# Tile starts at multiples of 64 bytes, and the delta rule's block transfers moved, in a four-layer decoder trunk on one core

## The chip, the cores and the metric

The kernel runs on one core of a Trainium2 chip. The metric is device time in microseconds of one execution. Before the change the median of three runs is 1248.63 us (1247.71 to 1249.18). The profile comes from one further execution, of 1247.2 us, whose instructions span 1245.1 us. Engines are named PE (matmuls; PEld is the weight load that overlaps them), DVE, ACT, POOL (GpSimd) and SP, which here only issues DMAs.

## The reference

The input is 256 positions of 1024 features in float32. Four layers follow; layer i uses mixer i mod 3 and then a convolutional feed-forward part, each with a norm before it and a residual sum after it:

```
for i in range(DEPTH):                       # DEPTH = 4
    h = rmsnorm(x, mix_norm[i])
    # i % 3: 0 = block attention, 1 = gated short convolution, 2 = gated delta rule
    x = x + mixer(h)
    x = x + conv_ffn(rmsnorm(x, ffn_norm[i]), w_up, conv_w, w_down)
return rmsnorm(x, final_norm)

def conv_ffn(h, w_up, conv_w, w_down):       # 1024 -> 2 x 2816 -> 1024
    u = causal_dwconv(h @ w_up, conv_w)
    return (silu(u[..., :FFN_DIM]) * u[..., FFN_DIM:]) @ w_down
```

So layers 0 and 3 are attention, layer 1 is the short convolution and layer 2 is the gated delta rule. In the delta rule each of 8 heads has queries, keys and values (after a convolution of width 4 and silu), and per chunk of positions it solves a unit lower triangular system:

```
a_mat = where(strict, (k_beta @ k.T) * decay, 0)
t_mat = triangular_solve(a_mat + eye, eye)   # the inverse
u, w = t_mat @ v_beta, t_mat @ (k_beta * exp(gc))
# then over the chunks, in order:
v_new = u_i - w_i @ state
o_i   = q_i @ state + a_i @ v_new
state = state * sd_i + k_i.T @ v_new
```

Its output is normalised per head, gated by silu(z) and multiplied by an output matrix.

## The kernel before

Activations stand transposed, features on partitions: `x` is 8 blocks of 128 features by 256 positions. The large matrix products keep float32 accuracy by splitting both operands into a rounded high part and the rest. A product of a weight tile with `x` is three matmuls (high x high, high weights x low, low weights x high). Where high and low activations stand side by side in one tile (`xs`, `aw`, `yw`), it is two: 512 columns against the high weights and 256 against the low ones. All operands of these are of the type that PE takes in one pass.

**The weights** come as one stream of 404 chunks of 8 tiles (128x128) each, in the order of use (class `Stream`, lines 104 to 168). SP issues the loads into four buffers `wraw`; ACT rounds a chunk to `whi` (line 152) and DVE takes the difference `wlo` (line 153), up to five chunks ahead of PE. All of SP's DMAs stand in one queue and are issued in its order: an issue that waits for a semaphore holds everything behind it, the weight loads too.

**The order of PE's work** is written out by hand by a planner (class `Weave`, lines 171 to 215). A `fill` generator brings the large products tile by tile, each tile adding 0.327 to the planner's clock. Beside it run steps, generators that yield a pair: what the PE work just emitted adds to the clock, and how much clock must pass, or which named events must be set, until the step goes on. Whatever is due is emitted after the current tile; where the fill has to wait for an event, the clock is moved on without PE work. PE executes exactly this order, and an instruction whose data isn't there holds all behind it. The order on the other engines and DMA queues is made by the framework's scheduler. The helper `after` (line 267) ties an instruction to the last emitted matmul in that scheduler, as an order only, without a semaphore.

**The delta rule** (function `gdn`, line 600) takes the heads in two halves of four. Its fill is 16 jobs of 16 tiles, `q0` to `q7` (queries and keys), then `v` (values) and `z` (gates) for two heads each, then the output product, which needs `o0` (first half's heads) for its first half and `o1` for its second. Each half runs through these steps:

- `lengths` (711): transposes of queries and keys, squares. It waits for `L_QK` after a head's activation.
- `systems` (745): the four heads' triangular matrices into `aq`. At its end SP stores their key part to DRAM (line 766).
- `invert` (775): SP reads the 16x16 diagonal blocks back as `bl` (781). POOL inverts them row by row into `xb` (789 to 794). SP stores `xb` to DRAM (796) and reads it back in another shape as `xc` (799). After `L_BLOCKS` and `L_JOIN` on the planner's clock DVE multiplies it into `xt32` (802). `xb` and `bl` have one buffer, so the second half's elimination follows the first's.
- `join16` (811) and `join_half` (848): DVE transposes 32x32 squares to `xi32` (809), PE joins inverse blocks to 32, 64 and 128 rows.
- the rest of `half` (941): two chunks are solved one after the other, with PSUM copied by ACT or DVE between the products; `finish` (917) normalises each chunk (ACT squares, POOL's root at 928, DVE's scaling at 931, PE's transposes, ACT's copy at 936), and `output` (999) gates and splits it for the output product.

The tiles are taken from pools in the order in which the code names them; a tile's size is its last dimension in bytes. The pool `keep` begins with `x`, `xh`, `xl`, then `pv`, `cs`, `half8`, `warm`, `idle`; the pools of the weights, of small temporaries and of each layer part come behind it.

Of the kernel before, what the change touches and what calls it, by code (L numbers as in the profile page):

```python
# [9 lines left out]
F32 = mybir.dt.float32  # L10
# [5 lines left out]
P = 128  # L16
# [4 lines left out]
H = 8  # L21
# [17 lines left out]
SCALED = 5  # L39
LAG = 1.75  # L40
L_HEAD, L_SOFTMAX, L_TURN, L_MIX, L_READY = 3.5, 9.0, 1.0, 2.5, 0.5
L_QK, L_V, L_LEN, L_SYS, L_BLOCKS, L_JOIN, L_XI, L_PM, L_OUT = 6.0, 6.0, 1.0, 0.5, 6.0, 13.0, 1.0, 2.5, 1.0


PV_MIX = 0
# [6 lines left out]
PV_N = PV_GN + 1  # L52
# [12 lines left out]
C_N = C_ST + 2 * H  # L65
# [153 lines left out]
def trunk(ctx: ExitStack, tc: tile.TileContext, xT, wstream, pvec, cst, wba, hv, out):  # L219
    nc = tc.nc  # L220
    V, S, G = nc.vector, nc.scalar, nc.gpsimd

    keep = ctx.enter_context(tc.tile_pool(name="keep", bufs=1))
    wpool = ctx.enter_context(tc.tile_pool(name="wpool", bufs=1))
    psum = ctx.enter_context(tc.tile_pool(name="psum", bufs=1, space=PSUM))
# [3 lines left out]
    xht = keep.tile([P, KB, T], F32R, name="xh")  # L229
    xlt = keep.tile([P, KB, T], F32R, name="xl")  # L230
    xh, xl = [[z[:, k, :] for k in range(KB)] for z in (xht, xlt)]
    pv = keep.tile([P, PV_N], F32, name="pv")
    cs = keep.tile([P, C_N], F32, name="cs")
    xg = []
    half8 = keep.tile([P, 2, 8], F32, name="half8")

    V.memset(half8[:, 0], -0.5)
    V.memset(half8[:, 1], 0.5)
    warm = keep.tile([P, 8], F32, name="warm")
    S.activation(warm, half8[:, 0], AF.Square)  # L240
    ws = Stream(nc, wpool, wstream, wstream.shape[0])
    nc.sync.dma_start(out=pv[:, :PV_SC], in_=pvec[:, :PV_SC])
# [24 lines left out]
    def after(inst):  # L267

        tc.add_manual_dep(inst.ins, PE.last.ins.name, mybir.DependencyInfo(
            mybir.DependencyClass.NoSync, mybir.DependencyReason.SCHED_ONLY), reason="a DMA's latency")  # L270
# [5 lines left out]
    def bank(tag, bufs=4):  # L276
        return psum.tile([P, 512], F32, name=tag, bufs=bufs)
# [322 lines left out]
    def gdn(gain):  # L600
        nm = Norm()
        NS = 2 * G_H
        with tc.tile_pool(name="gdn", bufs=1) as pool, \
# [8 lines left out]
            V.tensor_sub(ws2[:, :, 2 * H:], wb, ws2[:, :, :2 * H].bitcast(F32))  # L612
            bt = pool.tile([P, 2, H], F32, name="bt")
            g = pool.tile([P, 2, H], F32, name="g")
            gc = pool.tile([P, 3, H], F32, name="gc")
            dl = pool.tile([P, H], F32, name="dl")
            eg = pool.tile([P, H], F32, name="eg")
            neg = pool.tile([P, H], F32, name="neg")
# [2 lines left out]
            def big(dt=F32):  # L621
                return pool.tile([P, NS, P], dt, name="big", bufs=NB)
# [122 lines left out]
            def systems(s):  # L745

                s.aq = pool.tile([P, NS, 2, P], F32, name="aq", bufs=2)
                yield 0, (f"d{s.h0}",)
                for a in range(G_H):
                    y = s.y[a]  # L750
                    pk = bank("sm")
                    for t in range(2):
                        ts = slice(t * P, (t + 1) * P)
                        PE.matmul(pk[:, t * T:(t + 1) * T], lhsT=y[:, 1, ts], rhs=y[:, 0:2, ts],
                                  start=True, stop=True)
                    for t in range(2):
                        m = 2 * a + t
                        V.scalar_tensor_tensor(s.aq[:, m], pk[:, t * T:(t + 1) * T].rearrange(
                            "p (q i) -> p q i", q=2), s.sk[:, m:m + 1],
                            s.dt[:, a, t, :].unsqueeze(1).to_broadcast([P, 2, P]), op0=ALU.mult, op1=ALU.mult)  # L760
                    yield 0.87, 0.5 * LAG

                nb = P // BLK
                row = (BLK * P + BLK) * nb
                d1 = dram.tile([NS * row], F32, name="d1")
                nc.sync.dma_start(
                    out=d1.rearrange("(m x) -> m x", m=NS)[:, :P * P].rearrange("m (p c) -> p m c", p=P),
                    in_=s.aq[:, :, 1, :])
                s.d1 = d1

                s.am = big()
                V.tensor_mul(s.am, s.aq[:, :, 1, :],
                             cs[:, C_UP:C_UP + P].unsqueeze(1).to_broadcast([P, NS, P]))

            def invert(s):

                nb, d1 = P // BLK, s.d1

                bl = pool.tile([NS * nb, BLK, BLK], F32, name="bl", bufs=1)
                with nc.allow_non_contiguous_dma(reason="16 values of a block's row"):  # L780
                    nc.sync.dma_start(
                        out=bl, in_=d1.rearrange("(q y) -> q y", q=NS * nb)[:, :BLK * P]
                        .rearrange("q (j c) -> q j c", j=BLK)[:, :, :BLK])
                xb = pool.tile([NS * nb, BLK, BLK], F32, name="xb", bufs=1)
                xm = pool.tile([NS * nb, BLK, BLK], F32, name="xm", bufs=1)
                G.memset(xb, 0.0)
                G.memset(xb.rearrange("p j i -> p (j i)")[:, ::BLK + 1], 1.0)
                yield 0, L_BLOCKS
                G.tensor_scalar(xb[:, 0, 1:], bl[:, 0, 1:], -1.0, None, op0=ALU.mult)
                for k in range(1, BLK - 1):  # L790
                    n, r = k + 1, BLK - 1 - k
                    G.tensor_mul(xm[:, :n, :r], xb[:, :n, k:k + 1].to_broadcast([NS * nb, n, r]),  # L792
                                 bl[:, k:k + 1, k + 1:].to_broadcast([NS * nb, n, r]))
                    G.tensor_sub(xb[:, :n, k + 1:], xb[:, :n, k + 1:], xm[:, :n, :r])  # L794
                d2 = dram.tile([NS, nb, BLK, BLK], F32, name="d2")
                nc.sync.dma_start(out=d2.rearrange("m b j i -> (m b) j i"), in_=xb)
                xc = pool.tile([P, NS, BLK], F32, name="xc", bufs=1)
                with nc.allow_non_contiguous_dma(reason="16 values of a block's row"):
                    nc.sync.dma_start(out=xc, in_=d2.rearrange("m b j i -> (b j) m i"))
                s.xt32 = pool.tile([P, NS, 2, BLK], F32, name="xt32", bufs=2)  # L800
                yield 0, L_JOIN
                after(V.tensor_mul(s.xt32, xc.unsqueeze(2).to_broadcast([P, NS, 2, BLK]),
                                   cs[:, C_EO:C_EO + 2].unsqueeze(1).unsqueeze(3).to_broadcast([P, NS, 2, BLK])))
# [137 lines left out]
            def half(s):  # L941
                yield from lengths(s)
                yield 0, L_SYS
                yield from systems(s)
                yield from invert(s)
                yield from join16(s)
                yield from join_half(s, 32, (0, 64), (0,), lambda r, m: s.xi32[r, m, :],
# [87 lines left out]
    for l in range(DEPTH):  # L1035
        kind = l % 3
        subs.append((lambda g, l=l, kind=kind: moba(g) if kind == 0 else sconv(g) if kind == 1
                     else gdn(g), PV_FFN + l * KB))
        subs.append((lambda g, l=l: ffn(l, g), PV_MIX + (l + 1) * KB if l + 1 < DEPTH else None))
# [97 lines left out]
```

## Time and profile before

| | |
|---|---|
| median of three runs | 1248.63 us (1247.71 to 1249.18) |
| profiled execution | 1247.2 us |
| its span | 1245.1 us |
| PE busy | 1225.7 us, 98% of the span |
| PEld busy | 1127.5 us, 91% |
| DVE busy | 982.9 us, 79% |
| ACT busy | 775.5 us, 62% |
| POOL busy | 104.4 us, 8% |
| DMA | 215.80 MB, mean 173 GB/s |

The span's times count from its first instruction. Matmuls are pipelined: one that lasts 0.28 us starts some 0.12 us after the one before it, so the distance from start to start is what a stream of them costs, and PE counts as busy throughout. Idle time is listed with what ended it. The chain of work that ended last is followed back from the last instruction, at each step to what released it. The delta rule's part of the trace runs from about 578 us (its first tile) to 756 us (the last tile of its output product).

### The profile page before, as it was taken

The page shows a single profiled execution, that of the slowest core. Times are in us where ns is not written, and L with a number is a line of the kernel's source. Part 1 is how long each engine was busy: PE and PEld are TensorE (multiplying, and loading weights), DVE is VectorE, ACT ScalarE, POOL GpSimd, SP SyncE. Part 2 cuts the span into 40 slices and gives each one's busy share as a digit, 9 for nine tenths or more (in the row PEclk, how much of TensorE's full clock was granted, in tenths as well). Part 3 has the DMA queues.
Part 4 walks back from the last instruction along what each step waited for, and adds up shares of the span by engine and source line. Part 5 has one row for each costly group of instructions (what it writes and reads, how often), then busy time and mean ns, then how long its engine had stood idle before and what let it go on. Part 6 is the DMA issues. An engine that isn't in the chain of part 4 may idle for free.

```text
span 1245.1 us, 22068 instructions
## 1 busy us (share of the span) xinstructions
PE 1225.7 (98%) x8366; PEld 1127.5 (91%) x8366; DVE 982.9 (79%) x1720; ACT 775.5 (62%) x1427; POOL 104.4 (8%) x147
## 2 busy tenths in 40 slices
PE   9999999999999999999997999999999999999997
PEld 8989988889999988889997999988889989988886
DVE  6756999966878999866995668999775756999952
ACT  6655777644445777645873666777554655777641
POOL 2002000001002000001045102000011002000000
PEclk9999999999999999999998999999999999999998
DMA  8544465655555465655344244555655444466650
GB/s 289 200 153 166 146 201 186 213 188 189 176 182 186 153 201 193 200 189 183 126 131 126 90 136 137 200 192 189 208 190 175 156 161 165 145 202 188 211 177 34
DMA packets 67418, 215.80 MB, mean 173 GB/s; under 512 B 11248, under 2 KB 14832, under 8 KB 67312
## 3 DMA queue, kind: packets, MB, share of 16 engines
q1 hardware_dynamic: 67024, 213.86, 52.3%
q8 instruction: 66, 1.08, 0.3%
q10 hardware_dynamic: 288, 0.52, 0.1%
q14 instruction: 40, 0.33, 0.1%
HBM read 212.13 MB, written 2.23 MB: 172 GB/s over the span
## 4 chain that ended last, share of the span: by engine, by line
PE 89%; DVE 4%; ACT 2%; DMA 2%; issue 1%; POOL 1%; SPq 0%; POOLq 0%; DVEq 0%; ACTq 0%
PE mm L254 72%; PE sm L254 16%; DVE wlo L153 2%; DMA wraw<-wstream 1%; PE sm L257 1%; DVE xl L292 1%; ACT whi L152 1%; DVE yqk L422 1%; POOL xb L794 1%; POOL xm L792 1%; ACT jk L729 0%; DMA bl<-d 0%; DVE x L392 0%; DVE big L692 0%; DMA xc<-d 0%
## 5 line engine op out<-in xcount | busy, mean ns | idle before, releaser
L153 DVE TENSOR_TENSOR wlo<-wraw,whi 128x1024 fp32r<-128x1024 f32 (+1 forms) x404 | 489.5, 1212 | 155.7 <-ACT whi L152 154.0
L152 ACT CAST whi<-wraw 128x1024 fp32r<-128x1024 f32 (+1 forms) x404 | 420.2, 1041 | 290.9 <-PE mm L254 239.5
L254 PE MATMUL mm<-xh,whi 128*128 128x256 f32 x1024 | 296.5, 290 | 0.2 <-ACT whi L152 0.2
L254 PE MATMUL mm<-xh,wlo 128*128 128x256 f32 x1024 | 289.1, 282 | 1.2 <-DVE wlo L153 1.2
L254 PE MATMUL mm<-xl,whi 128*128 128x256 f32 x1024 | 288.7, 282 | 0.7 <-DVE xl L292 0.7
L254 PE MATMUL mm<-xs,whi 128*128 128x512 f32 x704 | 248.3, 394 | 0.0
L254 PE MATMUL mm<-aw,whi 128*128 128x512 f32 x704 | 247.3, 393 | 0.0
L254 PE MATMUL mm<-aw,wlo 128*128 128x256 f32 x704 | 199.1, 283 | 0.0
L254 PE MATMUL mm<-xs,wlo 128*128 128x256 f32 x704 | 199.1, 283 | 0.0
L254 PEld LDWEIGHTS mm<-xh,wlo 128*128 128x128 f32 x1024 | 193.5, 189 | 2.3 <-DVE wlo L153 2.1
L254 PEld LDWEIGHTS mm<-xl,whi 128*128 128x128 f32 x1024 | 193.8, 189 | 1.8 <-DVE xl L292 1.1
L254 PEld LDWEIGHTS mm<-xh,whi 128*128 128x128 f32 x1024 | 193.7, 189 | 1.4 <-ACT whi L152 0.4
L254 PEld LDWEIGHTS mm<-aw,whi 128*128 128x128 f32 x704 | 132.2, 188 | 30.6
L254 PEld LDWEIGHTS mm<-xs,whi 128*128 128x128 f32 x704 | 132.2, 188 | 30.5
L422 DVE SCALAR_TENSOR_TENSOR y<-u,pv,y 128x255 f32<-128x255 f32 (+1 forms) x352 | 149.0, 478 | 0.4
L254 PE MATMUL sm<-xs,whi 128*128 128x512 f32 x384 | 135.7, 393 | 0.0
L306 POOL TENSOR_TENSOR sq<-sq 128x256 f32<-128x256 f32 x62 | 53.3, 859 | 974.6 <-ACT sq L304 972.8
L254 PEld LDWEIGHTS mm<-xs,wlo 128*128 128x128 f32 x704 | 132.4, 188 | 0.0
L254 PEld LDWEIGHTS mm<-aw,wlo 128*128 128x128 f32 x704 | 132.3, 188 | 0.0
L254 PE MATMUL sm<-xs,wlo 128*128 128x256 f32 x384 | 108.6, 283 | 0.0
L420 ACT ACTIVATE y<-u,pv 128x256 f32<-128x256 f32 x176 | 81.4, 504 | 11.9 <-DVE u L451 6.6
L254 PEld LDWEIGHTS sm<-xs,whi 128*128 128x128 f32 x384 | 72.1, 188 | 16.6
(210 smaller groups left out, 1509.5 us busy)
## 6 DMA issues: line engine op xcount, KB each, us to landing
wraw<-wstream SPq DMA_DIRECT2D x396, 512.0 KB, 3.4
wraw<-wstream SPq DMA_DIRECT2D x8, 256.0 KB, 4.8
x<-xT SPq DMA_DIRECT2D x8, 128.0 KB, 4.7
d<-aq SPq DMA_DIRECT2D x2, 512.0 KB, 3.7
out<-xg ACTq DMA_DIRECT2D x2, 256.0 KB, 2.5
cs<-cst SPq DMA_DIRECT2D x1, 329.0 KB, 6.4
pv<-pvec SPq DMA_DIRECT2D x1, 324.5 KB, 4.9
cs<-cst SPq DMA_DIRECT2D x1, 320.0 KB, 5.9
```

What stands on the lines that cost most here:

```text
L152: self.nc.scalar.copy(hi[:, s], raw[:, s])
L153: self.nc.vector.tensor_sub(lo[:, s], raw[:, s], hi[:, s].bitcast(F32))
L254: self.last = nc.tensor.matmul(*a, **k)
L257: self.last = nc.tensor.transpose(*a, **k)
L292: V.scalar_tensor_tensor(xl[n], xn, col(gain + n), xh[n].bitcast(F32), op0=ALU.mult, op1=ALU.subtract)
L306: G.tensor_add(sums[0], sums[0], sq)
L420: S.activation(y, u, AF.Copy, scale=col(taps[0]))
L422: V.scalar_tensor_tensor(y[:, d:], u[:, :T - d], col(c), y[:, d:], op0=ALU.mult, op1=ALU.add)
L792: G.tensor_mul(xm[:, :n, :r], xb[:, :n, k:k + 1].to_broadcast([NS * nb, n, r]), bl[:, k:k + 1, k + 1:].to_broadcast([NS * nb, n, r]))
L794: G.tensor_sub(xb[:, :n, k + 1:], xb[:, :n, k + 1:], xm[:, :n, :r])
```

## The change

Sizes that put later tiles off a multiple of 64 bytes are rounded up to 16 floats (`even`): `pv`, `cs`, `warm`, and `gc` gets a fourth plane. In the delta rule POOL issues the store of its own rows instead of SP; the store of `aq` and the read of `xc` are tied to the last emitted matmul with `after`; two new yields, `L_STORE` and `L_ROWS + L_BACK`, stand before them on the planner's clock; and the constants change: `L_QK` 6.0 to 7.5, `L_XI` 1.0 to 2.0, `L_JOIN` 13.0 to 3.5, with the new `L_STORE` 2.0, `L_ROWS` 16.0, `L_BACK` 2.0.

```
-L_QK, L_V, L_LEN, L_SYS, L_BLOCKS, L_JOIN, L_XI, L_PM, L_OUT = 6.0, 6.0, 1.0, 0.5, 6.0, 13.0, 1.0, 2.5, 1.0
+L_QK, L_V, L_LEN, L_SYS, L_XI, L_PM, L_OUT = 7.5, 6.0, 1.0, 0.5, 2.0, 2.5, 1.0
+L_STORE, L_BLOCKS, L_ROWS, L_BACK, L_JOIN = 2.0, 6.0, 16.0, 2.0, 3.5
...
+    def even(n):
+        return -(-n // 16) * 16
...
-    pv = keep.tile([P, PV_N], F32, name="pv")
-    cs = keep.tile([P, C_N], F32, name="cs")
+    pv = keep.tile([P, even(PV_N)], F32, name="pv")[:, :PV_N]
+    cs = keep.tile([P, even(C_N)], F32, name="cs")[:, :C_N]
...
-    warm = keep.tile([P, 8], F32, name="warm")
+    warm = keep.tile([P, even(8)], F32, name="warm")[:, :8]
...
-            gc = pool.tile([P, 3, H], F32, name="gc")
+            gc = pool.tile([P, 4, H], F32, name="gc")[:, :3]
...
                     yield 0.87, 0.5 * LAG
+                yield 0, L_STORE
...
-                nc.sync.dma_start(
+                after(nc.sync.dma_start(
                     out=d1.rearrange("(m x) -> m x", m=NS)[:, :P * P].rearrange("m (p c) -> p m c", p=P),
-                    in_=s.aq[:, :, 1, :])
+                    in_=s.aq[:, :, 1, :]))
...
-                nc.sync.dma_start(out=d2.rearrange("m b j i -> (m b) j i"), in_=xb)
+                G.dma_start(out=d2.rearrange("m b j i -> (m b) j i"), in_=xb)
+
+                yield 0, L_ROWS + L_BACK
                 xc = pool.tile([P, NS, BLK], F32, name="xc", bufs=1)
                 with nc.allow_non_contiguous_dma(reason="16 values of a block's row"):
-                    nc.sync.dma_start(out=xc, in_=d2.rearrange("m b j i -> (b j) m i"))
+                    after(nc.sync.dma_start(out=xc, in_=d2.rearrange("m b j i -> (b j) m i")))
```

## Rows read from the trace of the kernel before

**Rows 1.** The page's part 4: shares by line of the chain that ended last.
```profile
PE mm L254 72%; PE sm L254 16%; DVE wlo L153 2%; DMA wraw<-wstream 1%; PE sm L257 1%; DVE xl L292 1%; ACT whi L152 1%; DVE yqk L422 1%; POOL xb L794 1%; POOL xm L792 1%; ACT jk L729 0%; DMA bl<-d 0%; DVE x L392 0%; DVE big L692 0%; DMA xc<-d 0%
```
**Rows 2.** Groups of PE by form: tiles, array, shapes, count, busy us, mean ns.
```profile
L254 PE MATMUL mm<-xh,whi 128*128 128x256 f32 x1024 | 296.5, 290 | 0.2 <-ACT whi L152 0.2
...
L254 PE MATMUL mm<-xs,whi 128*128 128x512 f32 x704 | 248.3, 394 | 0.0
...
L254 PE MATMUL sm<-xs,whi 128*128 128x512 f32 x384 | 135.7, 393 | 0.0
```
**Rows 3.** The chain in order of time, 680 to 860 us: start, us, what.
```profile
739.71 7.61 PE mm L254 x65
...
767.47 18.47 PE mm L254 x156
...
791.55 11.24 PE mm L254 x64
```
**Rows 4.** The chain in order of time, attention of layer 3, 1000 to 1045 us.
```profile
1005.51 7.00 PE mm L254 x30
...
1027.91 17.09 PE mm L254 x144
```
**Rows 5.** PE's waits, whole span: for what, us in total, times, longest.
```profile
PE sm L254 <- DVE xi L809: 5.7, 2, 5.1
...
PE sm L257 <- ACT yqk L707: 1.0, 1, 1.0
```
**Rows 6.** Waits of SP's DMA queue, whole span.
```profile
SPq L796 <- POOL xb L794: 25.3, 2, 14.9
...
SPq L781 <- DMA d<-aq: 6.6, 2, 4.0
```
**Rows 7.** Instructions of SP in order of time: start, us, issue.
```profile
634.68 0.38 SPq L766 DMA_DIRECT2D d<-aq  x1
...
658.05 0.49 SPq L796 DMA_DIRECT2D d<-xb  x1
```
**Rows 8.** Instructions of POOL, first half: the elimination's first and last of 29.
```profile
642.39 0.49 POOL L789 TENSOR_SCALAR xb<-bl 64x15 f32<-64x15 f32 x1 [10.83 <-DMA bl<-d]
...
657.78 0.24 POOL L794 TENSOR_TENSOR xb<-xb,xm 64x15 f32<-64x15 f32 x1
```
**Rows 9.** Busy time by window: window, length, PE, PEld, DVE, ACT, POOL, granted clock, DMA.
```profile
664.00:668.00 4.00, 3.82 (x18) 3.85 (x19) 2.23 (x5) 0.00 (x0) 0.00 (x0) 0.50 1.04 385
```
**Rows 10.** Instructions of PE: the first join's start and the second join's.
```profile
664.18 2.08 PE L254 MATMUL sm<-xi,big 128*128 128x16 f32 x9 [5.09 <-DVE xi L809]
...
693.82 1.85 PE L254 MATMUL sm<-xi,big 128*128 128x16 f32 x16
```
**Rows 11.** Instructions of PE in order of time, layer 1's feed-forward part.
```profile
560.31 0.39 PE L254 MATMUL mm<-aw,whi 128*128 128x512 f32 x1
...
560.65 0.40 PE L254 MATMUL mm<-aw,whi 128*128 128x512 f32 x1
```
**Rows 12.** The page's group of line 153, and line 772: durations min/median/max.
```profile
L153 DVE TENSOR_TENSOR wlo<-wraw,whi 128x1024 fp32r<-128x1024 f32 (+1 forms) x404 | 489.5, 1212 | 155.7 <-ACT whi L152 154.0
...
L772 DVE TENSOR_TENSOR big<-aq,cs x2: 1214/1220/1225, 635.2 to 664.8; 128x1024 f32<-128x1024 f32 x2
```
**Rows 13.** Window behind the second join, instructions with `xh` alone: PE first.
```profile
693.80:732.70 38.90, 19.50 (x93) 14.98 (x92) 0.00 (x0) 0.00 (x0) 1.00 0.25 82
```
**Rows 14.** Instructions of PE around the second half's last scores and transposes.
```profile
732.72 0.48 PE L254 MATMUL mm<-big,whi 128*128 128x256 f32 x2
...
739.46 0.48 PE L254 MATMUL mm<-big,whi 128*128 128x256 f32 x2
```
**Rows 15.** Instructions of POOL, the root of the last normalisation.
```profile
736.23 1.01 POOL L928 TENSOR_TENSOR f<-f,half 128x4 f32<-128x4 f32 x1 [9.56 <-DVE f L927]
```
**Rows 16.** Instructions of DVE: that normalisation's scaling, and the low part of the split.
```profile
737.47 0.69 DVE L931 TENSOR_TENSOR m<-m,f 128x512 f32<-128x512 f32 x1
...
742.15 0.69 DVE L416 TENSOR_TENSOR big<-z,big 128x512 fp32r<-128x512 f32 x1
```

## The prediction

> **What bounds the kernel now.** I read the page first. PE is busy in 98% of the span and the chain that ended last is 88% its matmuls on line 254 [rows 1]. So an edit pays in two ways only: by making a matmul of the stream shorter, or by removing one of the few places where PE stands still. DVE, ACT and POOL all have idle time.
>
> For the length of a matmul I took the chain in order of time, where an unbroken stretch divided by its count is the distance from start to start (the durations of [rows 2] overlap and can't be added). 156 matmuls from `xh`/`xl` take 18.47 us, 118.4 ns for 256 columns; 64 wide ones take 11.24 us, so a pair of 512 and 256 columns takes 351.2; the last product of the delta rule takes 7.61 / 65 = 117.1 [rows 3]. The value product of attention takes 7.00 / 30 = 233.3 ns for 512 columns, that is 116.7 per 256, and attention's last product 17.09 / 144 = 118.7 [rows 4]. 116.7 per 256 is the lowest mean of a stretch, and the other stretches lie 0.3% to 1.7% above it.
>
> For the places where PE stands I read its waits. The large one is on DVE's transposed block inverses, 5.7 us in two waits, the longest 5.1; another, 1.0 us, is on the activated keys [rows 5]. The second view is the delta rule's DMA queue. SP stands 25.3 us behind POOL's elimination before it can issue the rows' store [rows 6], in the first case until 658.05 [rows 7], because POOL eliminates from 642.39 to 658.02 [rows 8]. The weight loads queue behind that store. After PE's wait the granted clock is 0.50, the 1.2 GHz level, from 664 to 668, and the 18 matmuls there take 3.82 us [rows 9], 212 ns each, where the same product half a stage later takes 1.85 / 16 = 116 [rows 10].
>
> **Part 1, the tiles.** As the program before is laid out, tiles start at multiples of 32 bytes. `pv` (2884 bytes), `cs` (5192) and `warm` (32) leave everything behind them at 32 past a multiple of 64: the weight tiles, `aw`, `xs`, `oh`, `ol`, `yw`. `xh`, `xl` and the delta rule's `big` already stand at multiples of 64. Now all do. No instruction is added, `pv`, `cs`, `warm` and `gc` grow by 60, 56, 32 and 32 bytes.
>
> What it is worth is not in this trace: every matmul of the stream has at least one operand at 32. The nearest comparison says little for the starts alone. `xh` (aligned) and `oh` (not) both need 118.4 to 118.7 with the same weights; `big` (aligned) and attention's value product (moving tile not aligned) both reach about 116.7. So the start of the moving tile alone does not set the pace. What is left above 116.7 looks like an interplay of weight read and moving read, which new addresses can remove or bring. If all streams reach 116.7: 1856 pairs (704 + 384 from `xs` in [rows 2], as many as 704 from `aw` and 64 from `yw` by their loops) times 1.2 ns is 2.2 us, 3072 matmuls from `xh`/`xl` times 1.7 is 5.2, 384 from `oh`/`ol` (attention's output, 64 tiles x 3, twice) times 2.0 is 0.8; together 8.2 us gained. If the two streams at the floor fall to the others' 118.5, 192 times 1.8 plus 192 times 3.6 is 1.0 us lost. A further end: single pairs run faster than the mean, as the one from 560.31 to 560.65, some 0.345 us [rows 11]; were all like it, 1856 times 6 ns is 11 us, with the 256-column streams at the floor 17, and 20 with the value product. I take 4 gained, half of 8.2, and keep 1 lost and 20 gained. DVE and ACT should not notice: DVE's 1024-column subtraction of misaligned weights takes 1212 ns, its product on the aligned `big` 1220 [rows 12].
>
> The Trainium skill bears on this, in "SBUF — State Buffer", section "Specifications (TRN2)": a line there holds 16 bytes, and a new line costs. 32 is a multiple of 16 already, so by that page the new starts change nothing. No row here shows the line's size; the mechanism is my second rival below.
>
> **Part 2, the head of the delta rule.** What goes: the 5.7 us for the inverses, because the first join now stands 2 + 6 + 18 + 3.5 + 2 = 31.5 planner units behind the systems, where it stood 6 + 13 + 1 = 20. A tile is 0.327 units and 3 x 118.4 = 355 ns, so 31.5 units are 34 us. The chain itself needs less: from the block store's issue at 634.68 to the store of its rows are 23.4 us [rows 7], and the row read with DVE's multiplication and transposition adds 6: 29.5 to the join's first matmul, at 664.18 [rows 10]. With the wait goes the slow clock, 16 x 96 ns = 1.5 us, and with `L_QK` at 7.5 the 1.0 us on the keys. Sum 8.2 gained. If POOL's own store is slower than SP's 1.9 us (no row shows a POOL store), 31.5 units leave some 3 us of cover. One that takes 6 us more would bring back 3.
>
> SP no longer queues for POOL. Its two reads of blocks and rows still wait at its head for a store to land, the block read 4.0 us at most [rows 6], and weight loads queue behind that. POOL's store has no weight load behind it; the next elimination's clearing of `xb` waits for it, as it did before.
>
> **Part 3, the tail.** This is the price. Per half the planner's chain grows by 11.5, plus 1 for the second `L_XI`, plus 1.5 for `L_QK`: 14 units, 15 us. The filler for it comes from behind. After the second join the windows count 93 matmuls from `xh`, with those from `xl` 139, x 118.4 = 16.5 us [rows 13]. Before, these lay in the gaps of the last chains; now about 15 us of them go ahead of the join, and the last steps of both halves follow one another with only each other and the output product beside them. What then stands open is read from the second half: its last scores end where PE goes over to the output product, at 732.72; the squares, POOL's root at 736.23 and DVE's scaling, 737.47 to 738.16, follow, and the transposes could start then: 5.5 us. From the transposes' end at 739.46 to the start of DVE's share of the split at 742.15, where the first operand is there, another 2.7 [rows 14 to 16]. Beside the first gap stand some 2.6 us of PE work (the other half's last join, or what remains of the output's first half), beside the second nothing. Twice (5.5 - 2.6 + 2.7) is 11 us. That such a gap is planned at all shows in the planner's own sums: gone through with the new constants they end at 157.9 units against 149.4, and all of the difference is clock moved on without PE work. So: 4 us if the short hops close faster than these loaded ones, 11 by the rows, 14 if the clock falls after both waits as at 664. I take 8, between 4 and 11 and nearer to the rows, since ACT and DVE were partly busy with weights in the hops that I read.
>
> **Sum.** -4 - 8.2 + 8 = -4.2 us on the profiled execution's 1247.2 (span 1245.1): 1243.0. The median of the runs is 1.4 above that execution, so 1244.4.
>
> **The rivals.**
> 1. *The forecast*, 1239 to 1247, chance 0.39. For it: the 5.1 us wait, whose cause (SP held by POOL, filler too short) is edited directly. Against it: PE's filler is finite, so what leaves the head can return.
> 2. *The starts change nothing.* Then the delta rule decides alone, -8.2 + 8: 1248.4, between 1244 and 1252; chance 0.25. For it: `xh` and `oh` at one pace.
> 3. *All pairs at the short pace*, part 1 worth 15 to 20: 1248.6 - 20 + 0 = 1229 to 1234; chance 0.16. For it: single pairs already run at 0.345. Against it: 512 columns take exactly twice 256 in the other streams.
> 4. *The tail costs more than the head gives.* Place: PE between the last `z` tile and the output product's second half, waiting for DVE `f`/`big` and ACT's split. Price 14 against 8.2, with part 1 at 0 to 1 lost: 1248.6 + 6 = 1255, or 1251 with 11. It decides once PE idles there over 12 us (8.2 + 4). For it: the planner's own gap. Against it: hops with idle ACT and DVE are shorter than the loaded ones that I read. Chance 0.20.
>
> That the store from POOL does not free SP (the wait moved to the row read) would give back up to 5.7: 1250; it lies within 2 and 4.
>
> **How the numbers follow.** About 2.5 us, 0.2%, is what a measurement here can tell from no change. Case 1 is faster with 0.33 of its 0.39, case 2 is 0.08 faster, 0.12 same, 0.05 slower, case 3 faster, case 4 0.02 same and 0.18 slower. Faster 0.57, same 0.20, slower 0.23. The range 1230 to 1254 cuts off the outer end of cases 3 and 4. The forecast's own range is 1239 to 1249.
>
> **What would show it.** Right: matmuls from `xh` at 116.7 to 117.5, no wait on DVE `xi` over 1 us, no granted clock of 0.50 before 700, no SP wait on POOL, POOL waiting less than 3 us between elimination and next clearing; and new PE waits on DVE `m` and `big` after the last `z` tile, 8 us in sum. Wrong: pairs still at 351 (case 2) or at 345 (case 3); PE idle of over 12 us ahead of the output product (case 4); the first join still waiting.

## The result: 0.7% slower, and where the profile after shows it

The median after is 1256.38 us (1255.73 to 1259.97), against 1248.2 for the kernel before on the same chip. The ratio is 1.007, 95% interval 1.0057 to 1.0082. The forecast was 1244.4 with a range of 1230 to 1254: the kernel was to become faster, it became slower, and the time lies above the range. The profiled execution took 1256.95 us, its span 1255.1 (before 1247.2 and 1245.1).

The loss lies in one stage. Here are the delta rule's first product and the last matmul of its output product among PE's instructions, of the kernel before:

```profile
578.56 0.28 PE L254 MATMUL mm<-xh,whi 128*128 128x256 f32 x1
...
755.53 0.28 PE L254 MATMUL mm<-big,wlo 128*128 128x256 f32 x1
```

And the same two of the kernel after (its lines stand 7 to 10 further down):

```profile
578.74 0.27 PE L261 MATMUL mm<-xh,whi 128*128 128x256 f32 x1
...
764.67 0.28 PE L261 MATMUL mm<-big,wlo 128*128 128x256 f32 x1
```

From start to start that is 176.97 us before and 185.93 after, 9.0 more, of 10.0 in the whole span. The rest of the span grew by 1.0 us together. Busy time in the stage (window, length, PE, PEld, DVE, ACT, POOL, granted clock, DMA) for four kernels: before, e1 (the tiles alone, below), after, and e2 (the order alone, below):

```profile
578.56:755.65 177.09, 169.26 (x1522) 165.70 (x1521) 131.57 (x241) 115.84 (x263) 41.79 (x77) 0.98 0.41 128
...
578.27:757.24 178.97, 171.89 (x1523) 168.35 (x1521) 131.28 (x241) 115.68 (x262) 41.43 (x77) 0.96 0.40 127
...
578.74:764.79 186.05, 172.98 (x1523) 167.87 (x1521) 130.74 (x241) 117.01 (x264) 46.64 (x79) 0.95 0.38 122
...
577.74:767.31 189.57, 175.43 (x1522) 170.13 (x1521) 130.69 (x241) 116.84 (x263) 46.67 (x79) 0.94 0.39 120
```

Length less busy time is PE's idle time: 7.8 us before, 13.1 after. PE's busy time grew too, from 169.3 to 173.0 us, at a lower mean clock.

PE's waits after (for what, us in total, times, longest): of the 5.7 us on `xi` 0.5 is left, the 1.0 on the keys [rows 5] is gone, and 10.4 us in four waits have come. They are on `m`, the output that DVE has normalised, and on `big`, the part of the split that ACT rounds:

```profile
PE sm L264 <- DVE m L941: 6.2, 2, 3.7
PE mm L261 <- ACT big L422: 4.2, 2, 2.1
```

PE's instructions in order of time show where they stand: the first join, and then, for each half, the end of the last scores (713.42 to 714.41, and at 742.21), their transposes (721.65, 747.70) and the first matmul of the output product's half (724.84, 750.47). In brackets stands the wait before:

```profile
674.25 1.93 PE L261 MATMUL sm<-xi,big 128*128 128x16 f32 x16 [0.50 <-DVE xi L819]
...
713.42 1.16 PE L261 MATMUL sm<-m,aq 128*128 128x128 f32 x8 [0.32 <-ACT m L917]
714.41 0.60 PE L264 MATMUL sm<-cs,m 128*128 128x128 f32 x4
...
721.65 1.09 PE L264 MATMUL sm<-cs,m 128*128 128x128 f32 x4 [3.74 <-DVE m L941]
724.84 1.30 PE L261 MATMUL mm<-big,whi 128*128 128x256 f32 x2 [2.11 <-ACT big L422]
...
742.21 0.48 PE L261 MATMUL mm<-big,whi 128*128 128x256 f32 x2
...
747.70 0.66 PE L264 MATMUL sm<-cs,m 128*128 128x128 f32 x4 [2.42 <-DVE m L941]
750.47 1.30 PE L261 MATMUL mm<-big,whi 128*128 128x256 f32 x2 [2.11 <-ACT big L422]
```

The first join waits 0.50 us where it waited 5.09, and its 16 matmuls run at the pace of [rows 10]'s second join. So the head is repaired. Around it PE was busy 11.24 of 16 us before and 15.50 after:

```profile
660.00:676.00 16.00, 11.24 (x75) 11.10 (x76) 8.16 (x12) 3.22 (x5) 6.98 (x14) 0.79 0.67 204
...
660.00:676.00 16.00, 15.50 (x133) 15.32 (x132) 15.02 (x25) 10.26 (x17) 8.37 (x12) 1.00 0.68 186
```

The tail is the other way round. From 690 to the stage's end PE had no idle time before (first line); from 711 to the end 11.7 of 53.8 us are idle after. The windows behind show what the new waits cost beyond themselves:

```profile
690.00:755.65 65.65, 65.65 (x633) 64.86 (x632) 43.56 (x70) 41.91 (x94) 6.36 (x7) 1.00 0.37 121
...
711.00:764.79 53.79, 42.08 (x357) 39.89 (x355) 26.17 (x41) 26.71 (x61) 5.71 (x7) 0.84 0.21 69
...
719.00:724.00 5.00, 1.09 (x4) 0.72 (x4) 1.63 (x4) 0.87 (x3) 1.01 (x1) 0.50 0.02 3
724.00:728.00 4.00, 3.01 (x12) 2.72 (x13) 2.16 (x4) 1.24 (x2) 0.00 (x0) 0.50 0.00 0
...
745.00:750.00 5.00, 0.94 (x7) 0.49 (x5) 3.15 (x6) 2.09 (x5) 1.01 (x1) 0.95 0.36 115
750.00:754.00 4.00, 3.38 (x14) 3.10 (x15) 1.78 (x3) 1.03 (x2) 0.00 (x0) 0.50 0.31 119
754.00:765.00 11.00, 11.00 (x86) 11.00 (x86) 8.32 (x10) 7.09 (x14) 2.33 (x4) 0.89 0.29 97
```

In each half the clock falls to 0.50, the 1.2 GHz level: in the first half it is there from 719 on, inside the wait of 3.74 us, in the second it is still at 0.95 from 745 to 750 and at 0.50 behind the second wait. What that costs is an estimate from rows at either level. The output product takes 117.8 ns per matmul at the full clock in this trace (18 from 742.65 to 744.77): the 14 matmuls in 3.38 us lose 1.7 and the 86 in 11.00 lose 0.9. The 12 in 3.01 us are half of them 128 columns wide; eight such take 1.56 us there and 0.81 further on at the full clock, so these 12 lose some 1.7. The first half's four transposes take 1.09 us where four take 0.60 at 714.41, another 0.5. That is some 5 us in all. Idle time and clock together, the tail cost about 17.

The stream of matmuls itself did not get faster. The chain in order of time (start, us, what) has for the stretches of [rows 3]:

```profile
776.42 18.51 PE mm L261 x156
...
800.54 11.23 PE mm L261 x64
```

That is 118.7 ns per 256 columns from `xh`/`xl` (118.4 before) and 350.9 per pair (351.2).

On the DMA queue the change did what it says. SP waits for POOL nowhere any more; the row read now waits 7.9 us in two for POOL's store to land:

```profile
SPq L809 <- DMA d<-xb: 7.9, 2, 4.8
```

### The profile page after: what moved, and what is told of

It reads as the page before. It is cut to its first block, busy times and chain, and to the rows that moved or that the text cites. A ratio compares the mean times of both kernels' runs of the same rounds, so it can differ in the third digit from the quotient of the medians.

```text
span 1255.1 us, 22067 instructions
## 1 busy us (share of the span) xinstructions
PE 1231.2 (98%) x8366; PEld 1131.4 (90%) x8366; DVE 982.7 (78%) x1720; ACT 775.7 (62%) x1427; POOL 109.1 (9%) x149
## 4 chain that ended last, share of the span: by engine, by line
PE 88%; DVE 4%; ACT 2%; issue 2%; DMA 1%; POOL 1%; SPq 0%; POOLq 0%; DVEq 0%; ACTq 0%
PE mm L261 72%; PE sm L261 16%; DVE wlo L156 2%; DVE xl L299 1%; PE sm L264 1%; ACT whi L155 1%; POOL xb L802 1%; POOL xm L800 1%; DVE x L399 0%; DMA d<-xb 0%; DMA wraw<-wstream 0%; DMA bl<-d 0%; ACT jk L736 0%; ACT jk L935 0%; DVE z L1018 0%
## 5 line engine op out<-in xcount | busy, mean ns | idle before, releaser
L427 ACT ACTIVATE y<-u,pv 128x256 f32<-128x256 f32 x176 | 81.4, 504 | 13.1 <-DVE u L458 7.4
```

The source lines that it names most:

```text
L427: S.activation(y, u, AF.Copy, scale=col(taps[0]))
```

## The experiments

**e1_tiles: the tile starts alone.** The kernel before with these lines of the change and nothing else:

```
+    pv = keep.tile([P, even(PV_N)], F32, name="pv")[:, :PV_N]
+    cs = keep.tile([P, even(C_N)], F32, name="cs")[:, :C_N]
...
+    warm = keep.tile([P, even(8)], F32, name="warm")[:, :8]
...
+            gc = pool.tile([P, 4, H], F32, name="gc")[:, :3]
```

> The kernel before with only the tile sizes of the change (all larger tiles at multiples of 64 bytes). Theory A, the loss comes from the delta rule's order: this is within 1.5 us of before, 1247.5 to 1250, with pairs at 351 ns and matmuls from xh at 118.5 to 119.5, as in the trace after. Theory B, the new starts slow the stream of matmuls: 1253 to 1257, nearly the whole loss.

Measured 1249.4 us against 1248.57, ratio 1.0008 (0.9999 to 1.0017). The last 65 matmuls of the output product (`big`) are faster, 7.39 us, 113.7 ns; the 54 of it just before took 6.36, 117.8 each, and only four transposes stand between. The stretch from `xh`/`xl` is slower (118.7), attention's last product too (15.00 / 125 = 120.0 ns against 118.7 [rows 4]):

```profile
734.95 6.36 PE mm L258 x54
...
741.75 7.39 PE mm L258 x65
769.31 18.52 PE mm L258 x156
793.43 11.23 PE mm L258 x64
...
1030.08 15.00 PE mm L258 x125
```

So part 1 lost 0.8 us, by the interval between nothing and 2, and the delta rule's order carries the loss.

**e2_order: the order alone.** The kernel after, with the tile sizes of before (the lines of e1 the other way round).

> The changed kernel with the tile sizes of before, so only the delta rule's part of the change. Theory A: 1254 to 1257, PE waits on DVE m (normalisation) and ACT big (split) of some 10 us in the tail and a granted clock of 0.50 behind them. Theory B: 1247 to 1249.

Measured 1260.3, ratio 1.01 (1.0085 to 1.0116). The same two waits (6.2 and 4.2 us) stand in its trace, and one of 1.4 on `xi`. The order alone loses all that the change loses, and some 3 us more. Its trace tells part of why: in the stage's four lines above it has 1.1 us more idle time than the change and 2.4 us more busy time, and its clock is 0.62 from 676 to 680, behind the wait on `xi`, where the change has 1.00. Why the clock fell there was not tried.

**e3_early: the new order with a join as early as before.**

```
-L_STORE, L_BLOCKS, L_ROWS, L_BACK, L_JOIN = 2.0, 6.0, 16.0, 2.0, 3.5
+L_STORE, L_BLOCKS, L_ROWS, L_BACK, L_JOIN = 2.0, 6.0, 4.5, 2.0, 3.5
```

> The changed kernel with L_ROWS 4.5 in place of 16, so that the first join stands 20 planner units behind the systems, as before the change; POOL still issues its store. Theory A, a join that is put late takes the filler from the tail: the waits in the tail fall under 2 us, the wait for the inverses comes back with 3 to 7 us, 1246 to 1252. Theory C, the store from POOL and the tied transfers are themselves slow: the tail's end stays late, 1254 or more.

Measured 1253.72, ratio 1.0041 (1.0028 to 1.0055), above what was expected and just under theory C's 1254. The tail waits fell to 1.0 us, and the head wait is back, larger than before's 5.1:

```profile
PE sm L261 <- DVE xi L819: 8.0, 2, 6.8
```

SP now stands 18.6 us at the row read (longest 10.3), behind POOL's elimination by way of POOL's store: without the long yield, the block moves from the store to the read. So the first half of theory A stands (the filler is what moved); that this version would be as fast as the old order does not.

**e4_spstore: the rows' store back on SP,** in the kernel after.

```
-                G.dma_start(out=d2.rearrange("m b j i -> (m b) j i"), in_=xb)
+                nc.sync.dma_start(out=d2.rearrange("m b j i -> (m b) j i"), in_=xb)
```

> The changed kernel with the rows' store back on SP, all yields as after. Theory A, what counts is where the join stands, the issuing engine only frees SP: the tail's waits stay at 10 us or more, SP stands some 10 to 15 us behind POOL per half, weights come late and PE waits for whi or wlo by 1 to 6 us: 1255 to 1262. Theory C: the store from SP is quicker, 1249 to 1252.

Measured 1262.57, ratio 1.0114 (1.01 to 1.0128): 6 us slower than the change, just above the expectation. SP's wait is back, the tail waits are the same 6.2 and 4.2; PE's new waits are 2.1 us on `xi` and 1.7 on `u`, not the expected ones on weights:

```profile
SPq L804 <- POOL xb L802: 29.5, 2, 14.9
```

So POOL's store is not the cause of the loss; beside the long yields it gains about 6 us.

**e6_warm: the clock's share.** The kernel after, with 7 matmuls on zeros emitted ahead of each half's last transposes and 5 ahead of its output product, so that PE is busy in the tail waits (`keep_warm(n)` emits n matmuls of the zero tile `idle` with itself):

```
                 yield 0, 2 * LAG
+                if t == 1:
+                    keep_warm(7)
                 pt = bank("sm")
...
+                keep_warm(5)
                 wv.set(f"o{s.h0 // G_H}", L_OUT)
```

> The changed kernel with idle matmuls (a zero tile, result unused) in the tail's waits: 7 before the second normalisation's transposes of each half, 5 before each half's output may start, some 3 and 2 us at the full clock. Theory A with the slow clock as part of the price: no granted clock of 0.50 from 710 to 765, the output product at 113 to 120 ns throughout, 4 to 7 us less than after, 1249 to 1253, while the waits remain filled with idle work. Theory F, the waits alone are the price: 1255 to 1258.

Its windows, where the change has 0.50 and 0.89:

```profile
724.00:728.00 4.00, 3.66 (x25) 3.04 (x24) 2.47 (x4) 1.57 (x3) 0.00 (x0) 1.00 0.00 0
...
754.00:765.00 11.00, 11.00 (x96) 11.00 (x95) 10.72 (x14) 8.25 (x18) 3.85 (x5) 1.00 0.43 144
```

The clock stays at 1.00 throughout the tail, and the last window holds 96 matmuls where the change has 86. The profiled span is 1251.8, 3.3 us shorter. The timed runs don't confirm it: 1256.55, ratio 1.0072 (1.0049 to 1.0095), the same as after and within theory F's range. Two of its four runs have a mean clock of 0.997, and they took 1253.67 and 1256.27. That the waits pull the clock down is shown; that lifting it this way gives time in the median is not.

**e7_mid and e8_lout: moving the waits.** e7 takes the middle, with a join 25.5 units behind the systems; e8 lets the output product start later.

```
# e7
-L_QK, L_XI, L_ROWS = 7.5, 2.0, 16.0
+L_QK, L_XI, L_ROWS = 6.0, 1.0, 11.0
# e8
-L_OUT = 1.0
+L_OUT = 4.0
```

> The changed kernel with L_ROWS 11, L_QK 6 and L_XI 1: the first join stands 25.5 units behind the systems, between 20 and 31.5. Theory A, filler is taken from the tail one for one: the wait at the first join comes back with 1 to 4 us, the tail's waits fall to 3 us or less and the clock stays up, 1244 to 1250. Theory C, POOL's store and the tied transfers cost by themselves: 1252 or more.

> The changed kernel with L_OUT 4 in place of 1, so that the second half's first products stand ahead of the output product, which waits for the first half's split. Theory A: part of the tail's loss is that those products stand behind a matmul that waits; now the first output wait falls under 1 us and the second half's chain starts 2 to 4 us earlier: 1250 to 1255. Rival: the chain's own hops are the bound, and the waits only change places: 1255 to 1259.

e7: 1252.28, ratio 1.0035 (1.0022 to 1.0047), above theory A's range and within theory C's. It pays at both places, 3.7 us at the head and 3.1 in the tail:

```profile
PE sm L261 <- DVE xi L819: 3.7, 1, 3.7
PE mm L261 <- ACT big L422: 3.1, 1, 3.1
```

Behind both the clock is 0.50 (668 to 676, and 0.51 from 745 to 750), where theory A had it stay up; PE's idle time in the stage is 8.3 us, near the 7.8 of before. So its trace speaks for filler and clock. The ties by `after` were in every run with the new order; alone they were not tried, so theory C is not excluded for them.

e8: 1256.76, ratio 1.0063 (1.0047 to 1.0078), no gain, as the rival said; its waits only changed places:

```profile
PE sm L264 <- DVE m L941: 3.7, 1, 3.7
PE mm L261 <- ACT big L422: 3.1, 1, 3.1
PE sm L261 <- DVE xi L819: 1.6, 1, 1.6
```

**e5_shift: another distance between weights and moving tile.** The order of before and the rounded tiles, with every weight tile 64 bytes lower (`warm` is left out, `idle` takes its place) and a pad of 64 bytes behind them, so that the moving tiles stay where they were:

```
-    warm = keep.tile([P, even(8)], F32, name="warm")[:, :8]
-    S.activation(warm, half8[:, 0], AF.Square)
+    idle = keep.tile([P, T], F32, name="idle")
+    S.activation(idle[:, :8], half8[:, 0], AF.Square)
...
-    idle = keep.tile([P, T], F32, name="idle")
+    padb = tmp.tile([P, 16], F32, name="padb", bufs=1)
+    V.memset(padb, 0.0)
```

The distance from the weights to `xh`, `xl`, `oh`, `ol` and the wide tiles becomes 64 modulo 128 where it was 0; to `big` it becomes 0.

> The order of before, all larger tiles at multiples of 64 bytes, and only the weight tiles 64 bytes lower (the small tile ahead of them is dropped, 64 unused bytes stand behind them). So the distance of moving tile and weight tile, modulo 128, becomes 64 for xh, xl, aw, xs, oh, yw and 0 for big, where e1 had 0 for all and 64 for big. Theory D, the distance sets the pace: in e1 big with 64 ran at 113.4 ns and xh with 0 at 118.8 to 120, so now xh runs at 113 to 114, big at 118 to 120, which alone gives 14 to 19 us, and pairs fall from 351 to between 338 and 350: 1208 to 1236. Theory E, absolute addresses or a multiple of 64 bytes as such count: xh stays at 118 to 120, 1247 to 1251.

Measured 1243.43, ratio 0.9962 (0.995 to 0.9975): faster than before and than e1, but short of theory D's 1208 to 1236. In layer 0's feed-forward part `xh`/`xl` runs at 113.5 ns (17.70 / 156) where e1 has 118.7, attention's last product at 113.6 (10.79 / 95), and the delta rule's output product went back to 118.9 (7.73 / 65). The wide pairs, expected to fall, rose to 353.4 (11.31 / 32):

```profile
90.78 10.79 PE mm L258 x95
...
121.71 17.70 PE mm L258 x156
...
736.04 7.73 PE mm L258 x65
763.79 18.38 PE mm L258 x156
787.81 11.31 PE mm L258 x64
```

The same stretch of layer 2 (18.38) runs at 117.8, evenly from start to end and with no wait in it, from the same tiles `xh` and `xl`. So one stream can have two paces in one layout, as `big` had in e1 (113.7 and 117.8).

**e9_split: each stream at its better distance.** e5 without the pad behind the weights, so that `xs`, `aw` and `yw` move down with them (distance 0), `big` comes to 64, and a pad of 64 bytes in attention, meant to keep `oh` and `ol` at 64:

```
-    padb = tmp.tile([P, 16], F32, name="padb", bufs=1)
-    V.memset(padb, 0.0)
...
+            pad = pool.tile([P, 16], F32, name="pad")
+            V.memset(pad, 0.0)
             oh = pool.tile([P, H, T], F32R, name="oh")
```

> The order of before and whole multiples of 64 bytes, the weight tiles 64 bytes lower as in e5, but now every wide moving tile (xs, aw, yw) moves down with them, so that it keeps its distance of 0 modulo 128 to the weights, while xh, xl, oh, ol and the delta rule's output operand stand at a distance of 64. Theory D (the distance of moving and weight tile modulo 128 sets the pace, in opposite senses for single streams of 256 columns and for pairs of 512 and 256): the pairs return from 353.3 ns to 351.1, 1856 x 2.2 = 4.1 us; the delta rule's output product from 118.8 to 113.4, 192 x 5.4 = 1.0 us; 1243.4 - 5 = 1238, ratio 0.992. Rival (the pairs in e5 were slower for another reason, for instance more weight conversion beside a faster PE): pairs stay at 353, 1242 to 1243, with the output product at 113.4.

Measured 1237.92, ratio 0.9917 (0.9903 to 0.993). The three stretches that e5 and e1 show above are all at their better pace here, 113.7, 113.5 and 350.9. Others are not: attention's last product takes 118.0 (11.21 / 95), though it was to stay at e5's 113.6, after its first 24 matmuls, from the same tiles, had run at 114.1; and layer 2's stretch from `xh`/`xl`, at 117.8 in e5, is at 113.5. So that the time came out as expected to 0.1 us is in part luck:

```profile
91.05 11.21 PE mm L258 x95
...
733.29 7.39 PE mm L258 x65
760.78 17.70 PE mm L258 x156
784.10 11.23 PE mm L258 x64
```

**e10_gstore: POOL's store alone, on e9.**

```
-                nc.sync.dma_start(out=d2.rearrange("m b j i -> (m b) j i"), in_=xb)
+                G.dma_start(out=d2.rearrange("m b j i -> (m b) j i"), in_=xb)
```

> e9 with one thing more out of the change: POOL issues the store of its own rows, with no new yields and no ties, constants as before. Theory (the loss is the planner's new clock, not the store): SP's wait on POOL goes, the chain to the join stays as long (15 us elimination, store, read), so the first join's wait stays within 4 to 7 us and the delta rule's stage within 1.5 us of e9's; ratio to before within 0.002 of e9's. Rival (POOL's store is itself slow, or SP freed gives weights that the stream needed): the stage changes by 3 us or more.

Measured 1238.04, ratio 0.991 (0.9896 to 0.9924), the same as e9. The wait on `xi` is 5.2 us (e9: 5.9). SP is hardly freer: it stands 19.3 us at the row read, where in e9 it stood 25.1 at the store:

```profile
SPq L804 <- DMA d<-xb: 19.3, 2, 13.8
```

**e11_probe and e12_rows: the pace by place.** e1's kernel with streams of matmuls on zeros behind its end:

```
+    def stream(m, b, cols, n, w):
+        ps = bank("sm")
+        for i in range(n):
+            s = slice(w + i % 8 * P, w + (i % 8 + 1) * P)
+            PE.matmul(ps[:, :cols], lhsT=hi[:, s], rhs=m[:, b:b + cols], ...)
+            if cols > T:
+                PE.matmul(ps[:, :T], lhsT=lo[:, s], rhs=m[:, b:b + T], ...)
```

> The kernel with rounded tiles, and behind its end, as extra work that changes no output, streams of matmuls on zeros from tiles of known place: eight streams of 96 with 256 columns whose moving tile starts 0, 16, 32, ... 112 bytes behind the weight tile modulo 128 (weights at 0), eight of 48 pairs (512 with the first weights, 256 with the second) at the same distances, and four of 96 with 256 columns with the weights 64 bytes on and the moving tile at 0, 32, 64, 96. Theory D: 256 columns take 118 to 120 ns at distance 0, about 113.4 at 64, 116 to 119 at 32 and 96; the pairs 351 at 0 and 353 at 64; with the weights moved by 64 the order turns round (113.4 at moving 0, 119 at 64). Rival (the place of the moving tile alone, or of the weights alone, or other engines' traffic sets it): all distances alike, or the last four streams the same as the first at the same moving place.

> As e11, extra work on zeros behind the end, now on the one point that e11 left open: a distance of 64 modulo 128 gave 117.8 ns with the weights at 0 and the moving tile at 64, but 113.6 with the two exchanged. All tiles here are whole multiples of 512 bytes apart. Eight streams of 96 with 256 columns whose moving tile stands 0, 64, ... 448 bytes behind the weights modulo 512, the weights at a multiple of 128; the same eight with the weights 64 bytes on and the moving tiles unmoved; and eight of 48 pairs like the first eight. Theory D as it stands (the distance modulo 128 alone): places 0, 128, 256, 384 alike at 120, the four others alike near 113.5, in both series with the order turned round. Theory D2 (the distance modulo 512 counts): the four odd places differ among themselves by 2 ns or more, and the second series shows the same numbers one place on. Theory D3 (the absolute places count too): the second series is not the first one moved by a place.

Both ran once. In e12 each stream's first row gives its length; here the first five, 96 matmuls each, on weights at a multiple of 128 bytes, with the moving tile 0, 64, 128, 192 and 256 bytes further on:

```profile
1259.54 0.52 PE L258 MATMUL sm<-da,probehi 128*128 128x256 f32 x3
...
1271.06 0.40 PE L258 MATMUL sm<-db,probehi 128*128 128x256 f32 x2
...
1282.37 0.40 PE L258 MATMUL sm<-dc,probehi 128*128 128x256 f32 x2
...
1293.76 0.51 PE L258 MATMUL sm<-dd,probehi 128*128 128x256 f32 x3
...
1304.65 0.51 PE L258 MATMUL sm<-de,probehi 128*128 128x256 f32 x3
```

Start to start: 11.52, 11.31, 11.39 and 10.89 us, that is 120.0, 117.8, 118.7 and 113.5 ns per matmul. All streams of the two runs, ns per 256 columns, and per pair of 512 and 256:

```
e12, moving tile behind the weights' base, bytes   0      64     128    192    256    320    384    448
256 columns, weights at the base                 120.0  117.8  118.7  113.5  119.8  117.8  118.7  113.5
256 columns, weights 64 on                       117.7  120.0  117.8  118.6  117.8  119.9  117.8  118.6
pair, weights at the base                        347.0  353.3  350.9  353.1  353.2  353.3  350.9  353.3
e11, modulo 128                                    0      16     32     48     64     80     96     112
256 columns, weights at 0                          -    118.7  116.7  119.2  117.8  119.2  119.9  117.2
256 columns, weights at 64                       113.6         119.9         119.9         117.4
pair, weights at 0                               350.0  353.1  347.3  349.9  346.9  351.1  346.8  346.6
```

(The first stream of e11 began at the lower clock and is left out.) By its letter theory D3 holds: the second series of e12 is not the first one moved by a place, since no 113.5 is in it. But two facts of the kernel's own traces stand against reading the places alone from this table: a stretch keeps one pace from start to end, and the same tiles run at either of two (117.8 and 113.7 on the two sides of four transposes in e1, 117.8 and 113.5 in two layers of e5). By that, every stream of the table at a multiple of 64 fits the distance modulo 128 with two paces each: 113.5 to 113.6 or 117.7 to 117.8 at a distance of 64, 118.6 to 118.7 or 119.8 to 120.0 at 0. The streams of each series ran in the order of their places, so that they repeat every 256 bytes can also come from what ran before each. What picks the pace at a stretch's start was not tried: each place was only run behind streams of one and the same kind. The pairs follow another pattern. Of e11's expectation the turned order held (113.6 at moving 0, 119.9 at 64 with the weights moved by 64); the 113.4 at 64 did not (117.8), nor did the pairs (351 at 0 and 353 at 64; measured 350.0 and 346.9).

## Why the prediction was wrong

**The step that failed is the size of part 3, the tail.** It took 8 us, between 4 and 11, as "nearer to the rows", because ACT and DVE would be less loaded. The cost was about 17: 11.7 us of idle time and some 5 of clock. The mechanism and the places were right: PE idles between the last `z` tile and the output product, on DVE's `m` and on the split's first operand, twice. The prediction's own row-sum, 11 for the idle time, was good: the two kinds of wait measured 10.4, and short ones bring it to 11.7. From the last scores to their transposes it was 7.2 us in the first half and 5.5 in the second (5.5 was read), with 3.5 and 3.1 us of PE work beside them (2.6 was assumed); from the transposes' end to the first output operand 2.1 both times (2.7). So the step from 11 down to 8, that hops with idle engines are shorter, was the wrong one: in the first half ACT still serves the other half's last join between the squares, and that hop is longer than the one read. And the clock fell in both halves, some 5 us. The step had that price in it, too low (14 in all, "if the clock falls after both waits as at 664") and only as an upper bound, though the nearest row spoke for it: PE had waited 5.1 us there [rows 10] and run at 0.50 behind [rows 9]. With idle time foreseen in two groups of some 5 us, it belonged in the sum.

**Rival 4 came true**, place and direction; its price of 14 was 3 too low. It was to decide at over 12 us of idle with part 1 giving 4; the idle time was 11.7, but part 1 gave nothing.

**Part 1, the tiles, was also off: 4 taken, 0.8 lost** (e1, between nothing and 2), near the lower bound of 1 lost. Rival 2's number was right for this part, its reason was not: starts do matter, but not the multiple of 64. The prediction's phrase that the pace is an interplay of weight read and moving read held (e5, e9, e12). Its step from there to "half of 8.2" had nothing under it, since rounding all tiles up puts most streams in step with the weights (distance 0, 118.6 to 120.0), which is the slow place. The Trainium skill, "SBUF — State Buffer", section "Specifications (TRN2)", gives lines of 16 bytes. If only the place within such a line counted, places 64 bytes apart would be alike; e12 measures 113.5 to 120.0 between such places, so here the measurement decides.

**Part 2, the head, was right in mechanism and came out somewhat larger.** 8.2 was taken. The wait on `xi` went from 5.7 to 0.5 us, the keys' 1.0 went; all idle time up to the tail fell from 7.8 to 1.4. The clock is 1.00 from 660 to 676, where it was 0.79 in the mean. The prediction priced it for the 16 matmuls of the join alone, 1.5 us; in the trace before, the 13 matmuls from `xh` and `xl` behind them ran at 213 ns each too, and the clock cost some 3. That makes about 9.5. SP has no wait on POOL, and reads still wait for stores to land: the row read 4.8 us at most (4.0 foreseen, as the block read's bound). POOL's stores were in flight for a median of 3.8 us, against SP's 1.9; the cover of 31.5 units was enough.

**The fear in the last rival**, that POOL's store would only move SP's wait to the row read, is a small part of the change, whose yields bring the read into the queue late: there it waits 7.9 us in two, and PE's wait on `xi` is 0.5. Without the long yields it is what e3 and e10 show (10.3 and 13.8 us at the longest).

Added up: 9.5 gained at the head and 17 lost in the tail gives 7 to 8 lost, against the stage's 9.0; between 1 and 2 us are not accounted for. They are not the tiles: the stage of e1's profiled execution is 1.9 us longer than before, but it has less idle time (7.1 us against 7.8) and an output product that is in part faster. What it has more is clock at 0.50 behind the same wait on `xi`: its mean there is 0.50 from 668 to 672, where before has 0.68, and 0.88 from 676 to 690, where before has 1.00. So two single executions with nearly the same waits differ by some 2 us through the clock, and a difference of that size between two traces says nothing of the tiles. What else stays open: most of e2's extra 3 us, the ties by `after` alone, and whether the clock's 5 us are to be had (e6).

## What to carry to other kernels

Filler that is put in front of one wait is taken from behind another: PE's work is fixed, so go through the tail hop by hop with nothing beside it, and add the clock's fall behind each gap that is as long as one behind which the trace already shows it. Here every choice between the two ends (e3, e7, after) paid, and the old order paid least. Alignment for its own sake bought nothing; the places of the moving and the stationary tile together bought 0.8%, found by looking at the start-to-start pace of each stream, one by one. One stretch of a stream is not enough to judge a layout by: the same tiles ran at 113.5 and at 117.8 in one execution (e5).

## What the runs showed of the hardware

- The start-to-start pace of float32 one-pass matmuls went with the place of the two operands to each other: at the full granted clock 256 columns took 113.5 to 113.6 or 117.7 to 117.8 ns at a distance of 64 modulo 128, 118.6 to 120.0 at 0 (e11, e12). A stretch kept its pace from start to end, and the same tiles ran at either of two paces in one execution (113.7 and 117.8, e1; 113.5 and 117.8, e5); what picks one is open. Pairs of 512 and 256 columns ranged from 346.6 to 353.3 (e11, e12), with no rule found.
- In this kernel the better distances were 64 for the streams of 256 columns and 0 for the pairs (350.9 against 353.4): 10.3 us of 1248.2 in e9.
- In the kernel after, pairs of PE waits (3.7 and 2.1 us, 2.4 and 2.1 us) with four transposes between went with a clock of 0.50, in the first pair inside the first wait (from 719 to 728), in the second behind the second (from 750 to 754). With idle matmuls in the gaps the clock stayed at 1.00 (e6).
- Issuing the rows' store of 64 KB takes 0.64 to 0.77 us of POOL, and the store landed after a median of 2.1 us (e3) to 3.8 (after), two stores each; issued by SP it was 1.9 (before).
